# Latents loaded first, and the first three feature tiles multiplied in a written order

## The chip, the cores and the metric

The kernel runs on one core of a Trainium2 chip. Its engines have an instruction queue each: TensorE (PE, with a queue of its own for weight loads, PEld), VectorE (DVE), ScalarE (ACT), GpSimd (POOL) and SyncE (SP), which issues the loads. What is measured is the device time of one execution in microseconds (us).

## What is computed

Two layers of a backbone over 512 latent tokens and 256 context tokens, 1024 features wide, all in float32. Each layer begins with a normalisation that is modulated by a conditioning vector:

```python
shift, scale, gate = _adaln(c, ada_w[layer], ada_b[layer])
shift_c, scale_c, gate_c = _adaln(c_ctx, ada_w[layer], ada_b[layer])
h_l = _rmsnorm(x, norm_g[layer]) * (1.0 + scale[:, None]) + shift[:, None]
h_c = _rmsnorm(cx, norm_g[layer]) * (1.0 + scale_c) + shift_c
...
z = jnp.concatenate([h_c, h_l], axis=1) @ w_in
```

Layer 0 goes on with latent attention and a gated linear recurrence on z, layer 1 with neighbourhood attention. Only the start of layer 0 is touched here: the load of x and ctx, the two root-mean-squares, the modulation, and the first three 128-feature tiles of z.

## The kernel before

Features lie on the 128 partitions, tokens along the free axis: latents in columns 0 to 511 (`LAT`), context in 512 to 767 (`CTX`). The input is eight tiles `x_tiles[j]` of 128 x 768. Every matrix product is made of three float32r matmuls, high x high, high x low and low x high, so each operand is split in a high part (ACT copies) and a remainder (DVE subtracts); `split_raw` (L118 to L126) does that for weights.

The stage of the change goes in these steps.

`x_load` (L174) loads whole tiles; SP issues the loads in its queue's order. `norm0` (L356) squares each tile on ACT, adds the squares up in `acc0` on DVE, and at the last tile takes latents and context apart: `sq_sum` (L292) sums over the partitions on PE, `rs` (L311) makes the inverse root with one ACT root and five small DVE steps, `bc` (L318) broadcasts it by PE transposes, and ACT copies it to `rsb0`.

`ada_cols` (L242) makes modulation columns from weight chunks: `ada_mm` (L205) multiplies on PE (tile psada), ACT copies the rows, PE transposes them (psc), and DVE reduces and adds (`ashf`, `amul`). The first two input tiles have half chunks of their own (`ada_prep1`, `ada_go1`), the other six come in pairs from chunks 1 to 3 (`ada_prep`, `ada_go`), of which chunk ch needs the loads ch and ch + 4.

`hb(j, c)` (L403) makes the modulated input of tile j for latents (c = 0) or context (c = 1) by `h_block` (L335): DVE scales x by the column and the root, ACT adds the shift into `hh`, DVE takes the remainder `hl`.

`x_t(ft)` (L382) and `z_t` (L135) multiply: for each input tile k, three matmuls on the latents and three on the context, into one PSUM tile for each feature tile. psx0, psx1 and psg8 (weights w0t0, w0t1, w0t8) are the first three, psx2 (w0t2, started by the call behind this stage) is the fourth.

The order on each engine is made by a planner (`TC`, L20), which simulates the kernel and puts an instruction on its engine's queue when it is ready there, those written first going first. `behind(*engines)` (L198) pins what is written inside it behind the last instruction written so far on those engines. Buffers are tiles of pools: modulation weights have 8 (`t4a`), raw weights 3, their high parts and remainders 4 each.

Of the kernel before, what the change touches and what calls it, by code (L numbers as in the profile page):

```python
# [11 lines left out]
F32 = mybir.dt.float32  # L12
# [34 lines left out]
def build(nc, tc, A, out, dbg=None):  # L47
# [65 lines left out]
    def load_w(name, src, shape, new=None):  # L113
        raw = (new or t4)(name + "r", shape, F32, "r")
        SY.dma_start(raw, src)
        return raw
# [11 lines left out]
    def split_w(name, src, shape, new=None, eng=V, heng=S):  # L128
        return split_raw(name, load_w(name, src, shape, new), shape, new, eng, heng)

    def kfun(hl, n=None):
        h, l = hl
        return (lambda k: h[:, k], lambda k: l[:, k])
# [37 lines left out]
            for k in range(0, 8, step)  # L171
        ]

    def x_load(j):  # L174
        SY.dma_start(x_tiles[j], A["xin"][j])

    x_tiles = [px.tile([128, NT], F32, name=f"x{j}") for j in range(8)]
    ctt = cst.tile([128, 8, 2], F32, name="ctt")
# [19 lines left out]
    def behind(*engines):  # L198

        stack = ExitStack()  # L200
        for e in engines:
            stack.enter_context(tc.issue_after(next(i for i in reversed(nc.cur_bb.bb.instructions) if i.engine == e)))
        return stack
# [88 lines left out]
    def sq_sum(ps, sq, n, first, last):  # L292

        for i in range(0, n, 128):
            j = i // 64
            P.matmul(
                ps[:, j : j + 2], sq[:, i : i + 128], ones, start=(first and i == 0), stop=last,
                skip_group_check=True,
            )
# [26 lines left out]
    def rs_bc(name, ps, n, dst, pp, root=True):  # L326
        return bc(name, rs(name, ps, n, root), n, dst, pp)
# [21 lines left out]

    rsb0 = px.tile([128, NT], F32, name="rsb0")  # L350
    acc0 = px.tile([128, NT], F32, name="acc0")


    root = cst.tile([128, 1], F32, name="root")

    def norm0():  # L356
        sq = {}
        for j in range(8):
            sq[j] = th(f"sq{j}")
            S.activation(sq[j], x_tiles[j], AF.Square)  # L360
            if j == 4:
                S.activation(root, sq[0][:, 0:1], AF.Sqrt)
            for w in (LAT, CTX) if j == 7 else (slice(0, NT),):
                if j:
                    V.tensor_tensor(acc0[:, w], (acc0 if j > 1 else sq[0])[:, w], sq[j][:, w], ALU.add)
                if j == 7:
                    c = w is CTX
                    n, pp = (NL, NC)[c], (zz, zz3)[c]
                    ps = pp(f"pssum{c}")
                    sq_sum(ps, acc0[:, w], n, True, True)  # L370
                    if c == 0:
                        rs_bc("r00", ps, n, rsb0[:, w], pp)
                    else:
                        norm0c = lambda: rs_bc("r01", ps, n, rsb0[:, CTX], pp)
        return norm0c

    wt = {}

    def prep_t(ft):
        wt[ft] = kfun(split_w(f"w0t{ft}", A["w0t"][ft], (8, 128)))  # L380

    def x_t(ft):  # L382
        ps = zz(f"psx{ft}")
# [6 lines left out]
        ada_w[ch] = ada_load(0, ch, t4a)  # L390

    def ada_go(ch):
        for _ in ada_cols(0, 2 * ch, [ada_w.pop(ch), ada_w.pop(ch + 4)], paa):
            pass

    def ada_prep1(j):
        ada_w["half", j] = [[load_w(f"ada0{j}{m}", A["ada0"][j, m], (8, 128), t4a)] for m in range(2)]

    def ada_go1(j):
        for _ in ada_cols(0, j, ada_w.pop(("half", j)), paa, n=1):  # L400
            pass

    def hb(j, c):  # L403
        w = (LAT, CTX)[c]
        pc_ = [(lambda ap: ap, lambda ap: ap[:, w])]
        h_block(0, j, c, x_tiles[j][:, w], rsb0[:, w], hh[j], hl[j], pc_)
# [6 lines left out]
            going[key] = new  # L413
        next(going[key], None)

    psx = []
    for j in range(8):
        x_load(j)
    ada_prep1(0)
    norm0c = norm0()  # L420
    hh = [th(f"hh{j}", F32R) for j in range(8)]
    hl = [th(f"hl{j}", F32R) for j in range(8)]
    raw0 = load_w("w0t0", A["w0t"][0], (8, 128))
    ada_prep1(1)
    ada_go1(0)
    hb(0, 0)
    norm0c()
    with behind(PE, ACT):
        wt[0] = kfun(split_raw("w0t0", raw0, (8, 128)))
        hb(0, 1)  # L430
        ada_prep(1)
        ada_go1(1)
    hb(1, 0)
    hb(1, 1)
    ada_prep(5)
    ada_prep(2)
    ada_go(1)
    ada_prep(6)
    hb(2, 0)
    hb(2, 1)  # L440
    ada_prep(3)
    hb(3, 0)
    hb(3, 1)
    ada_prep(7)
    ada_go(2)
    hb(4, 0)
    hb(4, 1)
    ada_go(3)
    hb(5, 0)
    hb(5, 1)  # L450
    hb(6, 0)
    prep_t(1)
    hb(6, 1)
    hb(7, 0)
    hb(7, 1)
    prep_t(8)
    psx.append(x_t(0))
    psx.append(x_t(1))
    psg8 = zz3("psg8")
    z_t(both(psg8), wt.pop(8), hh, hl, 8)  # L460
    for j in range(8):
        dump(f"hh{j}", f(hh[j]))
        dump(f"hl{j}", f(hl[j]))
# [1375 lines left out]
```

## Time and profile before

| | us |
|---|---|
| median of 3 runs | 780.78 |
| lowest and highest run | 780.6, 781.55 |
| the profiled execution | 781.84 |
| its span, from first to last instruction | 780.0 |

One execution was recorded instruction by instruction. All times in rows are us from the start of the span, unless a row says ns. A line number is that of the program. A busy time says that an engine held an instruction, not that the instruction decided anything; what decides is read from the timelines, where "idle before" names what ended a wait.

### The profile page before, as it was taken

Reading aid. Unit: us, or ns where it says so; the run is one execution under the profiler, and the core shown is the slowest. Engines: PE = TensorE matmul, PEld = TensorE weight load, DVE = VectorE, ACT = ScalarE, POOL = GpSimd, SP = SyncE. Lnnn points to the kernel's source line nnn. Section 1 sums busy time; section 2 is a strip of 40 time slices with the busy share of each in tenths; the row PEclk is TensorE's granted clock in tenths of the full one; section 3 lists DMA queues with packets and bytes.
Section 4 is the critical chain, followed back from the end, with each engine's and each line's share of the span. In section 5 each row is a group of like instructions: output and inputs, shape, how many; then the busy total and the mean of one; then the engine's idle time right before and its main releaser. Section 6 shows DMA issues by size and latency. Waiting matters only on the chain.

```text
span 780.0 us, 13217 instructions
## 1 busy us (share of the span) xinstructions
PE 740.8 (95%) x4966; PEld 652.3 (84%) x4966; DVE 507.5 (65%) x1050; ACT 415.1 (53%) x810; POOL 164.8 (21%) x192
## 2 busy tenths in 40 slices
PE   2999999998999999999999999999999999999994
PEld 2678898887788877888998899889888799889994
DVE  5757599886478777653386467646653765568445
ACT  5434777954477777542344455445533644556533
POOL 0000002004154487404210023003200211022413
PEclk9999999999999999999999999999999999999998
DMA  8913413411455553256021541245125531436203
GB/s 322 408 58 109 134 50 100 165 39 38 118 155 158 166 160 119 89 196 236 28 82 59 149 145 29 82 125 173 59 78 162 166 105 55 111 100 169 82 1 108
DMA packets 33598, 95.29 MB, mean 122 GB/s; under 512 B 4608, under 2 KB 6784, under 8 KB 33536
## 3 DMA queue, kind: packets, MB, share of 16 engines
q1 hardware_dynamic: 32960, 93.93, 37.8%
q8 instruction: 39, 0.64, 0.3%
q10 hardware_dynamic: 576, 0.52, 0.2%
q14 instruction: 23, 0.19, 0.1%
HBM read 73.99 MB, written 4.19 MB: 100 GB/s over the span
## 4 chain that ended last, share of the span: by engine, by line
PE 75%; DVE 11%; ACT 5%; issue 3%; DMA 3%; SPq 1%; POOL 0%; DVEq 0%; ACTq 0%; POOLq 0%
PE psg L141 10%; PE psv L1270 8%; PE w0oy L1175 7%; PE psq L141 6%; PE w1oy L1175 6%; PE pskl L141 6%; PE psx L141 4%; PE pt L1387 3%; PE pskc L141 3%; PE s L808 3%; PE s L1346 2%; PE psada L215 2%; PE s L1347 2%; PE po L1370 2%; PE po L1371 2%
## 5 line engine op out<-in xcount | busy, mean ns | idle before, releaser
L764 POOL TENSOR_SCALAR p<-p,rc 128x512 f32<-128x512 f32 (+1 forms) x96 | 77.8, 813 | 323.7 <-DVE rc L763 309.7
L1354 ACT ACTIVATE p<-s,nm 128x512 f32<-128x512 f32 x64 | 43.8, 686 | 37.0 <-DVE nm L1352 20.9
L1390 DVE TENSOR_TENSOR ptl<-pt,pth 128x512 fp32r<-128x512 f32 x64 | 43.7, 688 | 26.7 <-ACT pth L1389 26.7
L1389 ACT ACTIVATE pth<-pt 128x512 fp32r<-128x512 f32 x64 | 37.3, 595 | 34.7 <-PE pt L1387 25.5
L1352 DVE CUSTOM_DVE_ANT_1 s<-s,bias 128x512 f32<-128x512 f32 x48 | 33.2, 696 | 16.5 <-PE s L1347 14.5
L1387 PE MATMUL pt<-ident,p 128*128 128x128 f32 x256 | 40.0, 272 | 0.0
L615 POOL TENSOR_TENSOR mix<-mix,la 128x256 f32<-128x256 f32 x4 | 3.6, 888 | 171.8 <-DVE la L609 123.6
L844 DVE TENSOR_TENSOR pt<-pt,pt 128x512 fp32r<-128x512 f32 x48 | 31.9, 681 | 11.5 <-ACT pt L843 11.3
L763 DVE RECIPROCAL rc<-rs 128x1 f32<-128x1 f32 x96 | 15.2, 158 | 32.7 <-ACT p L1354 23.6
L843 ACT ACTIVATE pt<-pt 128x512 fp32r<-128x512 f32 x48 | 27.4, 595 | 16.4 <-PE pt L881 16.2
L812 ACT ACTIVATE p<-s,nm 128x768 f32<-128x768 f32 x32 | 28.8, 901 | 11.7 <-DVE nm L810 11.5
L1346 PE MATMUL s<-k,q 128*128 128x256 f32 x128 | 34.3, 292 | 0.4 <-DMA q<-qx 0.2
L1387 PEld LDWEIGHTS pt<-ident,p 128*128 128x128 f32 x256 | 31.1, 140 | 4.0 <-issue 0.4
L810 DVE TENSOR_REDUCE nm<-s 128x1 f32<-128x768 f32 x32 | 30.4, 951 | 4.7 <-PE s L808 4.1
L1347 PE MATMUL s<-k,q 128*128 128x256 f32 x128 | 33.3, 284 | 0.0
L1370 PE MATMUL po<-pth,v 128*128 128x256 f32 (+1 forms) x96 | 31.7, 336 | 0.0
L1371 PE MATMUL po<-ptl,v 128*128 128x256 f32 (+1 forms) x96 | 29.6, 324 | 0.0
L881 PE MATMUL pt<-ident,p 128*128 128x128 f32 x192 | 28.7, 274 | 0.1
L862 PE MATMUL po<-pt,v 128*128 128x256 f32 x96 | 26.1, 296 | 1.9 <-DVE pt L844 1.8
L861 PE MATMUL po<-pt,v 128*128 128x256 f32 x96 | 26.6, 294 | 0.4 <-DVE rcc L763 0.4
L1346 PEld LDWEIGHTS s<-k,q 128*128 128x128 f32 x128 | 24.3, 190 | 3.1 <-issue 1.5
L1200 ACT ACTIVATE sq<-xr 128x512 f32<-128x512 f32 (+1 forms) x16 | 8.2, 522 | 33.1 <-DVE xr L1181 27.1
(966 smaller groups left out, 2635.3 us busy)
## 6 DMA issues: line engine op xcount, KB each, us to landing
ada_0r<-ada SPq DMA_DIRECT2D x22, 512.0 KB, 5.1
ada_4r<-ada SPq DMA_DIRECT2D x22, 512.0 KB, 5.4
q<-qx SPq DMA_DIRECT2D x32, 256.0 KB, 4.9
bias<-bias SPq DMA_DIRECT2D x16, 256.0 KB, 2.6
x<-xin SPq DMA_DIRECT2D x8, 384.0 KB, 6.4
xr<-xin SPq DMA_DIRECT2D x8, 384.0 KB, 7.0
x1d<-xr SPq DMA_DIRECT2D x8, 256.0 KB, 5.0
x<-x1d SPq DMA_DIRECT2D x8, 256.0 KB, 4.1
```

The source lines that it names most:

```text
L141: P.matmul(ps, a(k), b[k][:, c], start=(k == 0 and i == 0), stop=(k == nk - 1 and i == 2),)
L764: G.tensor_scalar(p, p, rc, 0.5, ALU.mult, ALU.mult)
L1175: P.matmul(ps, a, b[k][:, c], start=(n == m == 0 and ps is dst[0][0]), stop=(n == 7 and m == 2), skip_group_check=True,)
L1270: P.matmul(ps, tok(a[k], t), b[:, k % 4], start=(k == 0 and i == 0), stop=(k == 7 and i == 2))
L1346: P.matmul(s[:, :256], lhs, kap, start=(i == 0), stop=False, skip_group_check=True)
L1347: P.matmul(s[:, 256:], lhs, k2[:, CTX], start=False, stop=(i == 1), skip_group_check=True)
L1354: S.activation(p, s, AF.Exp, bias=nm, scale=-1.0, accum_out=rsum)
L1370: P.matmul(dst, vv, h, start=first, stop=False, skip_group_check=True)
L1371: P.matmul(dst, vv, l, start=False, stop=last, skip_group_check=True)
L1387: P.transpose(ps[:, 128 * j : 128 * j + 128], p1[hd, b][:, 128 * c : 128 * c + 128], ident)
L1389: S.activation(h, ps, AF.Copy)
L1390: V.tensor_tensor(l, ps, f(h), ALU.subtract)
```

## The change

Loads: the eight latent blocks (128 x 512) come first, then the weights of the first two modulation halves and of the first two feature tiles, and only then the eight context blocks (128 x 256), chunk 1 of the modulation, and the third feature tile's weights. Roots: `norm0` becomes two chains, one for the latents and one for the context, each with its own squares, adds, sums, root and broadcast; the context's squares get a tile of their own (`sqc`), and its sums lie in the PSUM slots of the modulation (`paa`). Matmuls: instead of `x_t` and `z_t`, which leave the order of the three feature tiles to the planner, `xk` multiplies one feature tile by named input tiles on latents or on context, and all of PE's work of this stage is pinned in the order in which it is written, the parts of the modulation in between (`go(key)` runs a modulation chunk to its next stop: first its matmuls, then its transposes).

```diff
+    def x_load(j, c):
+        w = (LAT, CTX)[c]
+        SY.dma_start(x_tiles[j][:, w], A["xin"][j][:, w])
...
+    def norm0(c):
+        n, w = (NL, NC)[c], (LAT, CTX)[c]
         for j in range(8):
-            sq[j] = th(f"sq{j}")
-            S.activation(sq[j], x_tiles[j], AF.Square)
...
+            sq = sqc[:, j] if c else th(f"sq{j}")[:, :NL]
+            S.activation(sq, x_tiles[j][:, w], AF.Square)
+            if j == 0:
+                prev = sq
+            else:
+                V.tensor_tensor(acc0[:, w], prev if j == 1 else acc0[:, w], sq, ALU.add)
+            if j == 0 and c == 0:
+                S.activation(root, sq[:, 0:1], AF.Sqrt)
+        ps = (zz, paa)[c](f"pssum{c}")
+        with behind(PE) if c else ExitStack():
+            sq_sum(ps, acc0[:, w], n, True, True)
+        r = rs(f"r0{c}", ps, n)
+        yield
+        with behind(PE):
+            bc(f"r0{c}", r, n, rsb0[:, w], (zz, paa)[c])
+        yield
...
+    def xk(ps, ft, c, js):
+        w, (wh, wl) = (LAT, CTX)[c], wt[ft]
+        with behind(PE):
+            for j in js:
+                for i, (a, b) in enumerate(((wh, hh), (wh, hl), (wl, hh))):
+                    P.matmul(
+                        ps[:, w], a(j), b[j][:, w], start=(j == 0 and i == 0), stop=(j == 7 and i == 2)
+                    )
...
     for j in range(8):
-        x_load(j)
+        x_load(j, 0)
     ada_prep1(0)
-    norm0c = norm0()
+    load0t(0)
+    ada_prep1(1)
+    load0t(1)
+    for j in range(8):
+        x_load(j, 1)
+    ada_prep(1)
+    ada_prep(5)
+    load0t(8)
+    n0, n1 = norm0(0), norm0(1)
+    next(n0)
+    go("h0", ada_go1(0))
+    go("h0")
+    next(n0)
...
+    with behind(DVE):
+        split0t(0)
     hb(0, 0)
...
+    go("h1", ada_go1(1))
+    go("h1")
     hb(1, 0)
...
+    split0t(1)
+    xk(psx[0], 0, 0, [0, 1])
+    xk(psx[1], 1, 0, [0, 1])
+    next(n1)
+    next(n1)
+    hb(0, 1)
     hb(1, 1)
-    ada_prep(5)
     ada_prep(2)
-    ada_go(1)
     ada_prep(6)
...
+    go("a1", ada_go(1))
+    with behind(DVE, ACT):
+        split0t(8)
+    xk(psx[0], 0, 1, [0, 1])
+    go("a1")
+    xk(psx[1], 1, 1, [0, 1])
...
+    for j in (2, 3):
+        for c in range(2):
+            hb(j, c)
+    for c in range(2):
+        xk(psg8, 8, c, [0, 1])
+    for i in (2, 3):
+        for c in range(2):
+            xk(psx[0], 0, c, [i])
+            xk(psx[1], 1, c, [i])
+        if i == 2:
+            go("a2", ada_go(2))
+    go("a2")
+    for c in range(2):
+        xk(psg8, 8, c, [2, 3])
+    for j in (4, 5):
+        for c in range(2):
+            hb(j, c)
+    go("a3", ada_go(3))
...
+    go("a3")
...
+    for i in range(2):
+        for c in range(2):
+            xk(psx[i], i, c, [6, 7])
+    for c in range(2):
+        xk(psg8, 8, c, [6, 7])
```

The lines left out multiply by input tiles 4 and 5 in the same manner, with chunk 3's transposes between the two.

## Rows read from the trace of the kernel before

**Rows 1.** The page: PE's busy us, share, instructions; its busy tenths by slice.
```profile
PE 740.8 (95%) x4966; PEld 652.3 (84%) x4966; DVE 507.5 (65%) x1050; ACT 415.1 (53%) x810; POOL 164.8 (21%) x192
...
PE   2999999998999999999999999999999999999994
```

**Rows 2.** Timeline of PE, 58 to 68: start, us, line, out<-in, count.
```profile
58.12 0.51 PE L141 MATMUL psg<-hh,w0t8l 128*128 128x512 f32 x2
58.75 0.58 PE L141 MATMUL psx<-hh,w0t2h 128*128 128x512 f32 x2
...
60.24 0.51 PE L141 MATMUL psx<-hh,w0t2h 128*128 128x512 f32 x2
...
67.66 0.35 PE L642 MATMUL psn<-w0n0h,hh 128*128 128x416 f32 x1
```

**Rows 3.** By stretch: length, busy (PE, PEld, DVE, ACT, POOL), PEclk, DMA share, GB/s.
```profile
23.30:28.80 5.50, 5.38 (x46) 3.06 (x47) 4.95 (x15) 2.86 (x7) 0.00 (x0) 1.00 1.03 401
28.80:35.00 6.20, 6.20 (x43) 4.15 (x43) 6.20 (x12) 3.10 (x5) 0.00 (x0) 1.00 1.03 411
35.00:43.00 8.00, 8.00 (x54) 5.94 (x53) 1.49 (x3) 1.28 (x2) 0.00 (x0) 1.00 0.86 344
```

**Rows 4.** Timeline of ACT and DVE, 9 to 21: squares, adds, root, its copy.
```profile
9.20 4.75 ACT L360 ACTIVATE sq<-x 128x768 f32<-128x768 f32 x5 [0.31 <-DMA x<-xin]
...
13.27 2.09 DVE L365 TENSOR_TENSOR acc<-acc,sq 128x768 f32<-128x768 f32 x3
...
17.49 0.27 ACT L304 ACTIVATE r00t<-pssumFalse,eps 128x4 f32<-128x4 f32 x1 [3.54 <-PE pssumFalse L296]
...
18.46 0.16 DVE L309 SCALAR_TENSOR_TENSOR r00r<-r00t,r00r 128x4 f32<-128x4 f32 x1
...
20.33 0.60 ACT L323 ACTIVATE rsb<-r00b 128x512 f32<-128x512 f32 x1 [0.74 <-PE r00b L322]
```

**Rows 5.** Timeline of DVE, 21 to 26: scaling, weight remainder, input remainder, columns.
```profile
21.72 1.15 DVE L338 SCALAR_TENSOR_TENSOR x<-x,am,rsb 128x512 f32<-128x512 f32 x2
...
22.79 1.22 DVE L125 TENSOR_TENSOR w0t0l<-w0t0r,w0t0h 128x1024 fp32r<-128x1024 f32 x1
...
23.92 1.14 DVE L341 SCALAR_TENSOR_TENSOR hl<-x,as,hh 128x512 fp32r<-128x512 f32 x2
...
24.98 0.17 DVE L234 TENSOR_REDUCE av<-psc 128x4 f32<-128x16 f32 x1
...
25.64 1.15 DVE L338 SCALAR_TENSOR_TENSOR x<-x,am,rsb 128x512 f32<-128x512 f32 x2
```

**Rows 6.** Timeline of PE: modulation halves, sums, broadcast, first feature matmul, chunk 1, transposes.
```profile
14.51 1.08 PE L215 MATMUL psada<-ada000r,c 128*32 128x128 f32 x16 [14.51 <-DMA ada000r<-ada]
...
15.52 1.87 PE L296 MATMUL pssumFalse<-ones,acc 128*128 128x2 f32 x8
...
19.18 1.12 PE L322 MATMUL r00b<-ident,r00r 128*128 128x128 f32 x4
...
21.60 0.61 PE L215 MATMUL psada<-ada011r,c 128*32 128x128 f32 x16
...
23.29 0.79 PE L141 MATMUL psx<-hh,w0t0h 128*128 128x512 f32 x2 [1.08 <-ACT hh L340]
...
24.11 0.64 PE L215 MATMUL psada<-ada_0r,c 128*32 128x256 f32 x8
...
24.57 0.61 PE L215 MATMUL psada<-ada_4r,c 128*32 128x256 f32 x8
...
46.61 0.38 PE L232 MATMUL psc<-ident,rows 128*128 128x128 f32 x2
```

**Rows 7.** DMA: packets from 7.5 to 12.5; one load (KB, us from issue to landing).
```profile
DMA packets 724, 2.03 MB, mean 406 GB/s; under 512 B 79, under 2 KB 79, under 8 KB 724
...
ada011r<-ada SPq DMA_DIRECT2D x1, 512.0 KB, 9.3
```

**Rows 8.** The scalings of x up to 60: ns least, median, most.
```profile
L338 DVE SCALAR_TENSOR_TENSOR x<-x,am,rsb x16: 476/612/752, 21.7 to 50.4; 128x512 f32<-128x512 f32 x8, 128x256 f32<-128x256 f32 x8
```

More of the change, by code (lines that the diff above doesn't have):

```diff
@@ L172, in ada_load @@
         ]
-    def x_load(j):
-        SY.dma_start(x_tiles[j], A["xin"][j])
+    def x_load(j, c):
+        w = (LAT, CTX)[c]
+        SY.dma_start(x_tiles[j][:, w], A["xin"][j][:, w])
     x_tiles = [px.tile([128, NT], F32, name=f"x{j}") for j in range(8)]
@@ L351, in build @@
     acc0 = px.tile([128, NT], F32, name="acc0")
+    sqc = px.tile([128, 8, NC], F32, name="sqc")
     root = cst.tile([128, 1], F32, name="root")
-    def norm0():
-        sq = {}
+    def norm0(c):
+        n, w = (NL, NC)[c], (LAT, CTX)[c]
         for j in range(8):
-            sq[j] = th(f"sq{j}")
-            S.activation(sq[j], x_tiles[j], AF.Square)
[L361 to L375, printed above, removed]
+            sq = sqc[:, j] if c else th(f"sq{j}")[:, :NL]
[14 more added lines that the diff above has]
+        yield
     wt = {}
@@ L392, in ada_go @@
     def ada_go(ch):
-        for _ in ada_cols(0, 2 * ch, [ada_w.pop(ch), ada_w.pop(ch + 4)], paa):
-            pass
+        return ada_cols(0, 2 * ch, [ada_w.pop(ch), ada_w.pop(ch + 4)], paa, True)
     def ada_prep1(j):
@@ L399, in ada_go1 @@
     def ada_go1(j):
-        for _ in ada_cols(0, j, ada_w.pop(("half", j)), paa, n=1):
-            pass
+        return ada_cols(0, j, ada_w.pop(("half", j)), paa, True, 1)
     def hb(j, c):
@@ L414, in go, with split0t, load0t @@
         next(going[key], None)
-    psx = []
+    def split0t(ft):
+        wt[ft] = kfun(split_raw(f"w0t{ft}", raw[ft], (8, 128)))
+    raw = {}
+    def load0t(ft):
+        raw[ft] = load_w(f"w0t{ft}", A["w0t"][ft], (8, 128))
     for j in range(8):
-        x_load(j)
+        x_load(j, 0)
     ada_prep1(0)
-    norm0c = norm0()
+    load0t(0)
[7 more added lines that the diff above has]
+    n0, n1 = norm0(0), norm0(1)
@@ L421, in build @@
+    next(n0)
+    go("h0", ada_go1(0))
+    go("h0")
+    next(n0)
     hh = [th(f"hh{j}", F32R) for j in range(8)]
     hl = [th(f"hl{j}", F32R) for j in range(8)]
-    raw0 = load_w("w0t0", A["w0t"][0], (8, 128))
-    ada_prep1(1)
-    ada_go1(0)
+    with behind(DVE):
+        split0t(0)
     hb(0, 0)
[L427 to L432, printed above, removed]
-    hb(1, 0)
+    go("h1", ada_go1(1))
@@ L434, in build @@
+    go("h1")
+    hb(1, 0)
+    psx = [zz("psx0"), zz("psx1")]
+    psg8 = zz3("psg8")
+    split0t(1)
[4 more added lines that the diff above has]
+    hb(0, 1)
     hb(1, 1)
-    ada_prep(5)
     ada_prep(2)
-    ada_go(1)
     ada_prep(6)
-    hb(2, 0)
-    hb(2, 1)
+    go("a1", ada_go(1))
[4 more added lines that the diff above has]
+    xk(psx[1], 1, 1, [0, 1])
     ada_prep(3)
-    hb(3, 0)
-    hb(3, 1)
@@ L444, in build @@
     ada_prep(7)
[L445 to L460, printed above, removed]
+    for j in (2, 3):
[9 more added lines that the diff above has]
+            go("a2", ada_go(2))
@@ new lines, in build @@
+    go("a2")
[6 more added lines that the diff above has]
+    for c in range(2):
+        xk(psx[0], 0, c, [4])
+        xk(psx[1], 1, c, [4])
+    go("a3")
+    for c in range(2):
+        xk(psx[0], 0, c, [5])
+        xk(psx[1], 1, c, [5])
+    for c in range(2):
+        xk(psg8, 8, c, [4, 5])
+    for j in (6, 7):
+        for c in range(2):
+            hb(j, c)
+    for i in range(2):
+        for c in range(2):
+            xk(psx[i], i, c, [6, 7])
@@ L461, in build @@
+    for c in range(2):
+        xk(psg8, 8, c, [6, 7])
+    wt.clear()
     for j in range(8):
```

## The prediction

> **What bounds the kernel now.** I began with the page's busy shares: TensorE (PE) is busy 95% of the span, and by the slices it is at 9 tenths everywhere but in the first [rows 1]. So an edit at the start is worth what it takes out of the first stage, if PE stays fed behind it. The stage ends, for my sum, where the fourth feature tile (psx2) does, since the first three and it are one unbroken run of PE work: at 67.66, with the first psn matmul [rows 2].
>
> The second view was busy time by stretch, around that start [rows 3]. From 23.3 PE is dense (5.38 of 5.5), and from 28.8 to 43 it has no idle time at all. In the same table VectorE (DVE) is the thing to watch: 4.95 of 5.5 from 23.3 and all of 6.2 from 28.8, and then 1.49 of 8 until 43. DVE is the second bound of this stage, hidden because PE always has something else queued.
>
> The timelines say what the start waits for. The squares on ScalarE (ACT) go at the pace of the input (five of 0.84 in 4.75), the adds on DVE end near 15.4 [rows 4], PE sums at 15.52, the inverse roots and their broadcast follow, the first modulation columns let DVE scale at 21.72, and the first feature matmul runs at 23.29 [rows 4 to 6]. Ahead of 14.51 PE does nothing.
>
> **The change, part by part.** *Loads.* 2.10 MB of latents replace 3.15 MB in front. The last whole tile landed by 13.1, where its square starts [rows 4]; the fourth had landed by 9.20, so 0.97 us a tile from there. By bytes, 2.10 MB is the end of the fourth tile and 1.3 more: 10.5. By number of rows moved (128 for each load, long or short) it would be up to 13.1. The queue moved 406 GB/s from 7.5 to 12.5, mostly with the same 3 KB rows [rows 7], and 401 to 411 later with 4 KB ones [rows 3], so bytes rule there: I take 11.0. Eight more issues of 0.33 to 0.5 us on SyncE (SP) are hidden: a load issued a little later landed 9.3 us after its issue [rows 7], the queue being full. If that cover went, 8 x 0.4 = 3 us would come back. [...]
>
> *Latent chain.* The 512-column add took 0.68 and the 256-column one 0.42 (2.09 for 768, 512 and 256 together, less 0.96) [rows 4]. Squares of 512 take some 0.6. Seven adds of 0.68 from 7.4 end at 12.2, against 14.9; PE can sum then (at 14.4 if the loads go by rows). In the written order PE then does sums (1.87), both halves of the first modulation columns (2 x 1.08 at this early pace, [rows 6]), the copy of the rows (0.3) and a transpose (0.42), and only then the broadcast (1.1). The columns are out on DVE by about 18.1, the broadcast copied by 19.1 (0.6, [rows 4]), against 21.7 and 20.9. A weight remainder, a scaling (below) and ACT's copy of 0.6 later the first feature matmul comes at 20.7, 2.6 earlier.
>
> *What DVE must do before chunk 1.* This is the step that decides. PE's order is now fixed: matmuls of input tiles 0 and 1 on latents for psx0 and psx1, then the sums of the context, its broadcast, and only then chunk 1's modulation matmuls, which before ran at 24.11 [rows 6]. The context sums therefore stand behind all of this on DVE, counted from 18.1 by start-to-start times [rows 5, 8]: two weight remainders of 1.13 (2.26); two scalings of 0.67 and two remainders of 0.67 (2.68; a latent and a context block together 1.07, split as their 0.75 and 0.48); the second columns (0.66); seven context adds of 0.42 (2.94). Sum 8.54. None can lie earlier: the first remainder is pinned behind the columns, the second weight lands past 18, and the context lands from about 18.7 to 21.3 (5.3 to 6.4 MB at 410 GB/s). So 26.6, with 0.3 of waits 26.9. The chain of the context then takes as long as it did: sums 1.0, root and five small steps 1.1, broadcast and its gap 0.8, 2.9 in all [rows 4 to 6]. Chunk 1 starts on PE at 29.8, although its data landed by 26. Moving its loads behind the context and the second weight therefore costs nothing; without that cover they would bind at 26.
>
> *PE from there.* One latent and one context matmul start 0.353 apart (21 such groups between 60.24 and 67.66) [rows 2]. Behind 29.8 lie 60 of those pairs (21.2), 12 context matmuls of 0.117 (1.4), three modulation chunks of 1.95 (four groups of eight, 0.46 apart) and three pairs of transposes of 0.35 (6.9) [rows 6]: 29.5. Holes: DVE starts chunk 1's columns behind two context blocks (0.2 at the context matmuls); the third weight's remainder (1.13) is pinned behind ACT's rows and comes out 0.7 after psg8 asks for it; input tile 2 needs its remainder, which the planner would again queue behind the scalings of two tiles (2 x 1.07), so 0.4 to 1.1 behind psg8's end. I take 1.3 for all. Before, PE filled such waits with any of the three tiles; the written order can't. For tiles 4 to 7 it leaves 4 us of other matmuls ahead, so no hole. The three tiles end at 60.6, against 58.45.
>
> *Given back.* psx0 ends 4.2 (12 pairs) before the stage does, and its weights' buffers go to the fourth tile, whose weights are then split in time. The 0.45 of gaps between its first matmuls (three groups took 1.49, [rows 2]) go: 24 pairs, 8.45. It ends at 69.05 against 67.66: **+1.4**. ACT gains 1.3 us of squares and DVE 0.9 of adds in all; ACT is idle half of that stretch (2.86 busy of 5.5, 3.10 of 6.2, [rows 3]). The root's table load stays behind the first square. The sums' new PSUM slots are shared with the columns, which are read by then. Nothing behind the fourth tile is edited, and PE's 95% [rows 1] lets the shift through.
>
> *The clock.* The 16 matmuls of half a load took 1.08 at 14.51 and 0.61 at 21.60 [rows 6], while the granted clock reads 1.00 in every stretch I read [rows 3]. Between 20.6 and 29.8 PE would now have about 5 us of work in 9. If it went back to the slow pace there, chunk 1 and what follows would take up to 1.7 longer. [...]
>
> **The rivals.** (1) *The early start carries through.* For: sums really come 3 us earlier, and if PE runs its columns at the later pace (0.95 less), DVE overlaps its list by 1 us, and the 1.3 of holes close, chunk 1 starts at 27.8 and 3.3 come back: 778.9. Against: the DVE list, which in the trace is as dense as can be [rows 3, 5]. It decides for a gain once chunk 1 starts before about 28.4. (2) *The latents land late, and slower for it.* Place: the first eight loads. If the queue goes by rows, they land at 13 instead of 11, and because every later step hangs on the first columns, all of the chain moves: +2.2 on the forecast, 784.4. It decides as soon as the last latent lands after 12, where DVE's adds no longer hide it. Against: the 406 GB/s with 3 KB rows. (3) *The clock falls* while PE waits for DVE: 783.9. (4) *The order changes nothing*, since the planner already mixes the three tiles [rows 2, 6] and PE was dense: then only the ends differ, 780.8.
>
> **How the numbers follow.** The profiled execution took 781.84, 1.84 more than its span of 780.0; the median of the runs shown is 780.78. Span 781.4, execution 783.2, and for the median 780.78 + 1.4 = 782.2. Own range: chunk 1 may start 1 earlier to 1.5 later, and holes 0.7 to 2, so 780.6 to 784. Chances: forecast 0.45, (1) 0.22, (2) 0.18, (3) 0.08, (4) 0.07. A measurement of this kernel tells about 0.2% (1.6 us) from no change: faster is below 779.2, slower above 782.3. The forecast lies almost on the second bound, so half of it counts as slower. Faster: most of (1), 0.20. Slower: 0.23 + 0.16 + 0.06 = 0.45. The rest, 0.35, is no change. The range takes in (1) and (2): 778.4 to 785.0.
>
> **What would show it.** In the changed profile: PE's first sums near 12 (loads by bytes) or 14 (by rows); first feature matmul near 20.7; DVE without a gap from 18 to 26.6; context sums on PE near 27 and chunk 1's modulation matmuls near 30; a hole of PE ahead of input tile 2's remainder; psx2's first matmul close on psg8's last, and its end near 69. I am wrong if chunk 1 runs before 28, which would mean that DVE's list was shorter or began earlier than counted, or if the shift at psx2's end isn't found at the end of the kernel.

## The result, and the profile after

The changed kernel took 791.56 us (median of four runs, 790.03 to 793.98) against 780.74 before: 1.0132 times as long, 95% interval 1.0113 to 1.0151. It is slower by 10.8 us, where 1.4 had been forecast. The four runs lie in two pairs, 790.0 twice and 793.08 and 793.98; the profiled execution is the last of these, with a span of 791.8 against 780.0.

Page of the changed kernel: busy us, share and instructions by engine; then PE's busy tenths and the granted clock in 40 slices. (PEld is TensorE too: the profile counts its weight loads in a row of their own.)

```profile
PE 746.8 (94%) x4966; PEld 658.9 (83%) x4966; DVE 508.1 (64%) x1056; ACT 416.3 (53%) x818; POOL 164.8 (21%) x192
...
PE   3799999899899998999999999999999999999994
...
PEclk9699999999999999999999999999999999999998
```

PE executes the same 4966 instructions as before and is busy 6.0 us longer [rows 1]; its low digits lie in the first two slices, up to 40 us, and so does the 6 of the clock. The PE timeline gives the chain of the start.

```profile
12.77 1.84 PE L297 MATMUL pssum<-ones,acc 128*128 128x2 f32 x8 [12.77 <-DVE sp L565]
...
21.57 0.33 PE L233 MATMUL psc<-ident,rows 128*128 128x128 f32 x1 [1.46 <-ACT rows L228]
21.66 0.48 PE L390 MATMUL psx<-hh,w0t0h 128*128 128x512 f32 x1
...
25.21 0.80 PE L390 MATMUL psx<-hh,w0t0h 128*128 128x512 f32 x1 [2.61 <-ACT hh L341]
...
29.16 0.63 PE L390 MATMUL psx<-hh,w0t1l 128*128 128x512 f32 x1
29.58 0.85 PE L297 MATMUL pssum<-ones,acc 128*128 128x2 f32 x4
31.73 0.66 PE L323 MATMUL r01b<-ident,r01r 128*128 128x128 f32 x2 [1.30 <-DVE r01r L310]
32.31 1.08 PE L216 MATMUL psada<-ada_0r,c 128*32 128x256 f32 x8
...
41.91 0.50 PE L390 MATMUL psx<-hh,w0t0h 128*128 128x512 f32 x1 [0.77 <-ACT hh L341]
43.27 0.50 PE L390 MATMUL psx<-hl,w0t0h 128*128 128x512 f32 x1 [0.86 <-DVE hl L342]
```

The sums come at 12.77 (15.52 before, [rows 6]) and the first feature matmul at 21.66 (23.29), so the early start is real. Then PE waits from 22.6 to 25.2 for the high part of input tile 1, works through nine latent matmuls (0.43 apart from the third on), and chunk 1's modulation begins at 32.31, 8.2 us later than before. The matmuls are long, 0.63 us and modulation groups of 1.08 where [rows 6] have 0.64: the stretches show why.

Stretches of the changed kernel; columns as in [rows 3], of which PE's busy time (first pair) and PEclk (third number from the end) matter.

```profile
19.50:22.20 2.70, 1.24 (x15) 0.76 (x8) 2.68 (x6) 2.70 (x9) 0.00 (x0) 1.00 1.02 338
22.20:25.20 3.00, 0.41 (x2) 0.00 (x0) 2.86 (x10) 1.57 (x4) 0.00 (x0) 0.77 1.00 367
25.20:29.20 4.00, 3.98 (x9) 2.81 (x10) 1.08 (x3) 0.00 (x0) 0.00 (x0) 0.50 1.01 373
29.20:32.30 3.10, 1.80 (x8) 1.33 (x6) 0.71 (x5) 0.26 (x1) 0.00 (x0) 0.50 1.03 403
32.30:37.50 5.20, 5.20 (x40) 3.00 (x40) 1.76 (x4) 2.71 (x6) 0.00 (x0) 0.50 0.99 375
37.50:43.00 5.50, 3.90 (x22) 2.75 (x20) 5.13 (x11) 2.57 (x5) 0.00 (x0) 1.00 0.96 336
43.00:50.00 7.00, 6.73 (x48) 4.55 (x49) 1.67 (x4) 0.70 (x2) 0.00 (x0) 0.76 0.23 91
```

PE is busy 0.41 of 3 us from 22.2, and in that stretch the granted clock falls from 1.00 to 0.50. It stays there until about 37.5, and falls again (0.76 from 43 to 50) behind the next holes (3.90 busy of 5.50), those ahead of input tile 2. Every stretch of [rows 3] read 1.00. In that first stretch the mean of 0.77 puts the fall near 23.8, 1.2 us into the wait.

The first psn matmul (psn is the product that follows psx2) stands at 76.6 instead of 67.66 [rows 2]: 8.9 us of the 11.8 by which the spans differ. The rest arises far behind, at 145 us. PE's waits there for lgl, the remainder of a gate's weights in the recurrence, between 136 and 152, first of the kernel before, then of the changed one (us in total, times, longest):

```profile
PE pg L141 <- DVE lgl L565: 0.8, 1, 0.8
```

```profile
PE pg L141 <- DVE lgl L617: 3.2, 1, 3.2
```

No line of that part was edited. VectorE has its work in another order there: the planner had another start to go by.

### The profile page after: what moved, and what is told of

It is laid out like the page before. It is cut to its first block, busy times and chain, and to the rows that moved or that the text cites. A ratio compares the mean times of both kernels' runs of the same rounds, so it can differ in the third digit from the quotient of the medians.

```text
span 791.8 us, 13243 instructions
## 1 busy us (share of the span) xinstructions
PE 746.8 (94%) x4966; PEld 658.9 (83%) x4966; DVE 508.1 (64%) x1056; ACT 416.3 (53%) x818; POOL 164.8 (21%) x192
## 4 chain that ended last, share of the span: by engine, by line
PE 77%; DVE 12%; ACT 5%; issue 3%; DMA 2%; POOL 0%; SPq 0%; DVEq 0%; ACTq 0%; POOLq 0%
PE psg L141 9%; PE psv L1322 8%; PE w0oy L1227 7%; PE psq L141 6%; PE w1oy L1227 6%; PE pskl L141 6%; PE pt L1439 3%; PE psada L216 3%; PE pskc L141 3%; PE s L860 3%; PE psx L390 3%; PE psx L141 2%; PE s L1398 2%; PE s L1399 2%; PE po L1422 2%
## 5 line engine op out<-in xcount | busy, mean ns | idle before, releaser
L1406 ACT ACTIVATE p<-s,nm 128x512 f32<-128x512 f32 x64 | 43.8, 686 | 37.4 <-DVE nm L1404 20.7
L1442 DVE TENSOR_TENSOR ptl<-pt,pth 128x512 fp32r<-128x512 f32 x64 | 43.6, 687 | 26.4 <-ACT pth L1441 26.3
L1404 DVE CUSTOM_DVE_ANT_1 s<-s,bias 128x512 f32<-128x512 f32 x48 | 33.3, 696 | 16.6 <-PE s L1399 14.5
L815 DVE RECIPROCAL rc<-rs 128x1 f32<-128x1 f32 x96 | 15.2, 158 | 31.8 <-ACT p L1406 21.6
L864 ACT ACTIVATE p<-s,nm 128x768 f32<-128x768 f32 x32 | 28.9, 902 | 11.3 <-DVE nm L862 11.1
L1423 PE MATMUL po<-ptl,v 128*128 128x256 f32 (+1 forms) x96 | 29.6, 324 | 0.0
L1398 PEld LDWEIGHTS s<-k,q 128*128 128x128 f32 x128 | 24.3, 190 | 3.2 <-issue 1.7
```

Source lines behind the costliest of these rows:

```text
L1398: P.matmul(s[:, :256], lhs, kap, start=(i == 0), stop=False, skip_group_check=True)
L1404: V.tensor_tensor_reduce(sv, sv, bb, -1.0, 3e38, ALU.add, ALU.min, nm)
L1406: S.activation(p, s, AF.Exp, bias=nm, scale=-1.0, accum_out=rsum)
L1442: V.tensor_tensor(l, ps, f(h), ALU.subtract)
```

## The experiments

Twelve further runs were made; e5_again is the change once more, unaltered. All are read by the same marks of their profiled execution: the start of chunk 1's modulation, the first psn matmul, the stretch from the last psn matmul to the first of pskr (transposes of psn's result; the stretch holds the wait for lgl), and the mean granted clock from 20 to 50. The column "before" is the median of the kernel before in the same series of runs.

| run | us | before | ratio, 95% | chunk 1 | psn | psn to pskr | clock 20 to 50 |
|---|---|---|---|---|---|---|---|
| kernel before | 780.78 | | | 24.1 | 67.7 | 64.3 | 1.00 |
| the change | 791.56 | 780.74 | 1.0113–1.0151 | 32.3 | 76.6 | 68.0 | 0.72 |
| e2_chains | 786.59 | 781.44 | 1.0049–1.0082 | 29.3 | 73.6 | 64.4 | 0.83 |
| e3_order | 787.98 | 781.44 | 1.0066–1.0096 | 31.4 | 72.4 | 67.9 | 0.89 |
| e4_chunk1 | 792.11 | 781.44 | 1.0119–1.0150 | 30.2 | 74.8 | 67.7 | 0.83 |
| e1_filled | 788.74 | 781.44 | 1.0078–1.0108 | 31.0 | 71.5 | 67.0 | 0.94 |
| e7_warm | 788.69 | 781.94 | 1.0061–1.0120 | 31.7 | 72.3 | 68.0 | 1.00 |
| e5_again | 789.64 | 781.71 | 1.0069–1.0113 | 32.5 | 76.9 | 66.5 | 0.72 |
| e8_lgl | 786.18 | 781.94 | 1.0038–1.0071 | 32.2 | 72.8 | 64.4 | 0.89 |
| e11_before_lgl | 781.66 | 781.71 | 0.9988–1.0007 | 24.0 | 67.5 | 62.8 | 1.00 |
| e6_adds | 788.59 | 781.94 | 1.0068–1.0114 | 31.3 | 71.9 | 66.6 | 0.89 |
| e10_pesum | 787.28 | 781.71 | 1.0057–1.0117 | 30.7 | 72.8 | 64.3 | 0.83 |
| e9_all | 786.95 | 781.94 | 1.0042–1.0075 | 31.3 | 71.9 | 64.1 | 1.00 |
| e12_best | 789.42 | 781.47 | 1.0093–1.0129 | 29.9 | 70.4 | 65.2 | 0.94 |

### Which part of the change costs: e2, e3, e4

**e2_chains** keeps the new loads and the two root chains, and leaves the order of all matmuls to the planner.

```diff
-    xk(psx[0], 0, 0, [0, 1])
-    xk(psx[1], 1, 0, [0, 1])
...
+    for ps, ft in ((psx[0], 0), (psx[1], 1), (psg8, 8)):
+        z_t(both(ps), wt[ft], hh, hl, 8)
```

> The first half of the change alone: latents loaded first and the two root chains, but the three feature tiles, the modulation and the roots in the order that the planner finds, nothing pinned. Clock theory and order theory: PE always finds some feature matmul, no wait over 2 us, psx2 ends at 66 to 69, time 779 to 782. Load theory (the split loads and the late context are what costs): psx2 ends at 73 or later, time 787 to 791.

Measured: 1.0065 times the kernel before. The planner's order leaves the same hole. PE timeline:

```profile
23.27 0.50 PE L141 MATMUL psx<-hh,w0t0h 128*128 128x512 f32 x1 [3.06 <-ACT hh L341]
23.61 0.40 PE L141 MATMUL psx<-hh,w0t1h 128*128 128x512 f32 x1
26.36 1.02 PE L297 MATMUL pssum<-ones,acc 128*128 128x2 f32 x4 [2.36 <-DVE acc L367]
```

PE waits 3.06 for ACT and 2.36 for the context's adds, and the granted clock reads 0.50 from 24 to 34. Split loads and a split norm lose time without the written order: 5.9 us at psn's start.

**e3_order** keeps the loads and the one norm of the kernel before, and has the written order alone.

```diff
     for j in range(8):
-        x_load(j, 0)
+        x_load(j)
     ada_prep1(0)
+    norm0c = norm0()
...
-    next(n0)
+    hb(0, 0)
+    norm0c()
```

> The second half alone: whole tiles loaded first and one chain of squares as in the kernel before, but the first three feature tiles and chunks 1 to 3 in the written order. Clock theory: both blocks of input tiles 0 and 1 are there by 28 and chunk 1's data by 24, so PE waits under 2 us at a time, the clock stays up, psx2 ends at 68 to 70, time 781 to 784. Order theory: as the changed kernel, psx2 at 74 or later, time 787 to 791.

Measured: 1.0081. Here the context's root is in time, but the written order waits too (26.74, 1.75 us for input tile 1, where the planner of the kernel before had run chunk 1), the clock is at 0.50 from 26 to near 33, and the stretch from psn to pskr is the long one. So neither part is harmless, and both have a wait of PE ahead of chunk 1.

```profile
26.74 0.79 PE L388 MATMUL psx<-hh,w0t0h 128*128 128x512 f32 x1 [1.75 <-ACT hh L340]
```

**e4_chunk1** is the change with chunk 1's modulation matmuls ahead of the context's sums.

```diff
     xk(psx[1], 1, 0, [0, 1])
+    go("a1", ada_go(1))
     next(n1)
     next(n1)
...
-    go("a1", ada_go(1))
```

> The changed kernel with chunk 1's modulation matmuls put ahead of the context's sums on PE. Clock theory: the wait at 22.2 stays as it is, the clock falls at 25 all the same, chunk 1 runs at the slow pace but 3 us earlier; psx2 ends at 73 to 76, time 787 to 791. Order theory (chunk 1 behind the context's chain is what costs): psx2 ends at 70 to 72, time 784 to 786.

Measured: 792.11 (790.68 to 792.69), no gain and above both ranges. In the profiled run, the fastest, chunk 1 starts 2.1 us earlier, and psn 1.8 earlier than in the profiled change, which by what e5_again shows below says little. Behind it the context's sums come at 32.13 instead of 29.58, and PE then waits 1.30 for the root and 1.53 for the first context block. The wait is moved, not removed: what is late is the context's chain, whichever of the two goes first.

### The clock: e1, e7, e5

**e1_filled** adds 25 unused matmuls where PE waits.

```diff
+    def warm(ps, n):
+        with behind(PE):
+            for _ in range(n):
+                P.matmul(ps, wt[0][0](0), hh[0][:, LAT], start=True, stop=True, skip_group_check=True)
...
-    xk(psx[0], 0, 0, [0, 1])
+    xk(psx[0], 0, 0, [0])
+    warm(psg8[:, LAT], 11)
+    xk(psx[0], 0, 0, [1])
```

> The changed kernel with 25 matmuls added that nothing uses, put into three places where PE only waits: 11 between input tiles 0 and 1 of psx0, 7 between the context's sums and its broadcast, 7 ahead of input tile 2. They keep PE at work and move nothing else. Clock theory (PE waits 3.0 us for DVE at 22.2, its clock falls to the lower level, and all its work runs at half pace from 25 to 37): granted clock 1.00 up to 40, psx2's last matmul ends at 69 to 71 instead of 76.6, time 783 to 787. Order theory (the written order itself leaves PE without work, the clock is a side show): psx2 ends at 75 or later, time 789 or more.

Measured: 1.0093 (788.74), psn at 71.5, both between the two theories. The clock fell all the same:

```profile
19.50:22.00 2.50, 0.67 (x11) 0.46 (x4) 2.50 (x5) 2.50 (x8) 0.00 (x0) 1.00 0.89 263
22.00:26.00 4.00, 4.00 (x12) 3.19 (x11) 3.84 (x13) 1.75 (x5) 0.00 (x0) 0.57 1.00 376
26.00:30.00 4.00, 4.00 (x21) 3.31 (x20) 0.79 (x5) 0.26 (x1) 0.00 (x0) 1.00 1.00 362
```

PE held matmuls without a gap from 21.6, and the clock was low from about 22.6 to 26; the wait that went ahead of it was that for the second columns (busy 0.67 of 2.50). I took the first wait to count as well as the one that I had filled.

**e7_warm** fills that one too, with matmuls that need only the first weights (29 unused ones in all).

```diff
+    warm(psg8[:, LAT], 6)
     go("h1")
```

> The changed kernel with 29 unused matmuls of 128 x 512 added on TensorE where it waits: 6 behind the second modulation half, 11 ahead of input tile 1, 5 between the context's sums and their broadcast, 7 ahead of input tile 2; they read only the first weights, so they can run from 19.9 on. Clock theory: the granted clock stays at 1.00 from 20 to 50; chunk 1's modulation starts near 30.5 and takes 1.9 instead of 3.6; psn's first matmul near 70 (76.6 without the fillers, 71.5 with the earlier fillers that still let the clock fall at 22.8), the later stall of the fourth gate remainder stays (about 3 us of wait instead of 0.8), in all 785 to 787 us. Rival (the written order and the late chain cost by themselves, whatever the clock): psn at 73 or later, 789 us or more.

Measured: the granted clock is 1.00 from 20 to 140, and yet psn starts at 72.3 and the kernel takes 1.009 times the time before. Part of the expectation held (chunk 1's modulation takes 1.9 instead of 3.6 us) and its size did not: with the clock kept up, psn is still 4.6 us later than in the kernel before, of 8.9. The fillers themselves are the measure of the holes (PE timeline):

```profile
22.60 0.27 PE L233 MATMUL psc<-ident,rows 128*128 128x128 f32 x1
...
23.41 2.69 PE L437 MATMUL psg<-w0t0h 128*128 128x512 f32 x11
26.81 0.50 PE L390 MATMUL psx<-hh,w0t0h 128*128 128x512 f32 x1 [0.72 <-ACT hh L341]
...
29.55 0.50 PE L297 MATMUL pssum<-ones,acc 128*128 128x2 f32 x4
29.91 1.40 PE L437 MATMUL psg<-w0t0h 128*128 128x512 f32 x5
31.35 0.41 PE L323 MATMUL r01b<-ident,r01r 128*128 128x128 f32 x2
31.69 0.64 PE L216 MATMUL psada<-ada_0r,c 128*32 128x256 f32 x8
```

Chunk 1 starts at 31.69 although every matmul from 20 on runs at a granted clock of 1.00: PE waits for VectorE and ScalarE, and here the faster PE only waited longer. The holes are 3.4 us ahead of input tile 1 (2.6 in the profiled change), 1.4 ahead of the broadcast (1.3) and 1.9 ahead of input tile 2's remainder (1.6).

The 4.6 are not all the kernel's own. The latents' sums began at 13.34 here (and in e8), 0.6 later than in the profiled change. And the fillers delay what they measure: the transpose of the second columns waits behind six of them until 22.60, though ACT had copied its rows by 22.1, VectorE then reduces these columns behind two adds, and input tile 1's scaling comes at 25.26 instead of 23.66, 1.0 later than the late begin explains. With both set off, I estimate that some 3 us of the 8.9 would remain at a clock that never falls. (In e1, whose sums began at 12.74 and whose clock was low for 3.4 us, 3.8 remain.)

**e5_again** is the change unaltered.

> The changed kernel unaltered, once more. Its four runs lay in two pairs, 790.0 and 793 to 794 us, and the profiled one was of the upper pair; the mend behind the fourth tile (which alters nothing ahead of 120 us) showed a granted clock that rose again at 30 us instead of 37.5, and psn's first matmul at 72.8 instead of 76.6. Theory (the same program falls into two courses of the clock in this stage, some 3.5 us apart): a profile of the lower course would show psn at 72.5 to 73, one of the upper at 76 to 77, and the runs lie near 790 and near 793.5 again. Rival (the two pairs are noise of another place): psn at 76.6 whatever the run takes.

Measured: 793.11 in the profiled run, 788.23 to 789.89 in four others. The profile is again of the upper pair's kind (psn at 76.9, mean clock 0.72 from 20 to 50). Of the nine runs of the change three took 793 to 794 us, with a mean granted clock of 0.981 or 0.982 over the whole span, and six took 788.2 to 790.0, with 0.987 to 0.989. So the two groups are two courses of the clock, upper and lower. No profile of the change itself fell in the lower one; but e8_lgl, which has the same instructions ahead of 120 us, ran through a lower course:

```profile
22.80:25.80 3.00, 0.38 (x3) 0.01 (x1) 2.86 (x10) 1.55 (x4) 0.00 (x0) 0.55 0.98 354
25.80:30.00 4.20, 4.20 (x9) 3.03 (x10) 1.06 (x3) 0.00 (x0) 0.00 (x0) 0.51 1.02 369
30.00:34.00 4.00, 2.71 (x39) 1.55 (x38) 1.83 (x8) 1.43 (x4) 0.00 (x0) 1.00 1.03 408
34.00:43.00 9.00, 7.07 (x42) 5.47 (x38) 7.49 (x16) 4.42 (x8) 0.00 (x0) 1.00 1.02 406
43.00:50.00 7.00, 7.00 (x71) 5.24 (x74) 2.38 (x8) 1.39 (x3) 0.00 (x0) 1.00 0.16 61
```

The clock falls sooner here, near 23.1 by the mean of 0.55, just as the wait begins (23.8 in the profile of the change), and it is up again at 30 instead of 37.5 and doesn't fall a second time. That is 3.8 us at psn's start (72.8 against 76.6), and the groups of the change's runs are 3 to 6 us apart. The sizes agree in the clock too: 0.72 against 0.89 over 30 us is 5.1 us of full clock, which over 790 us makes 0.0065, about what lies between 0.981 and 0.988. That the change's faster runs went through just this course of e8 is likely from these sizes, and not shown.

The price of the low clock is read against e7, where it read 1.00 from 20 to 140. As the rows stand, it is 0.5 us in the lower course (psn at 72.8 against 72.3), since PE would have waited for VectorE anyhow, and 4.3 in the upper. With e7's own delays set off (1.0, and for the upper course the late begin of 0.6 too) I estimate 1.5 and 5.9. The clock came up again at 30 in e8, where PE had been busy 4.20 of 4.20 us from 25.8, and at 37.5 in the change, busy 5.20 of 5.20 from 32.3. What decides between the two courses is not shown.

### Behind the fourth tile: e8, e11

**e8_lgl** pins one later step behind lgl; nothing ahead of 120 us is altered.

```diff
+        last_lgl[:] = [i for i in nc.cur_bb.bb.instructions if i.engine == DVE][-1:]
...
-    nat_norm(0)
+    with tc.issue_after(last_lgl[0]):
+        nat_norm(0)
```

> The changed kernel with the third normalisation of the token-wise part (nat_norm(0)) pinned on its engines behind the remainder lgl of the fourth gate, so that lgl leaves VectorE about 2 us earlier; nothing ahead of 120 us is touched. Theory (a part of the loss arises behind the fourth tile, from another planned order): the wait of TensorE for lgl falls from 3.2 to about 1.2 us and the dip of the clock behind it goes; pskr comes 2 to 3 us earlier than the 191.2 of the changed kernel, in all 788.5 to 789.5 us. Rival (the stall only moves, because VectorE or ScalarE is late there anyway): 791 to 792 us.

Measured: 786.18, better than expected; its four runs lie close together (785.87 to 787.35), where those of the change lie in pairs. PE's wait:

```profile
PE pg L141 <- DVE lgl L619: 1.4, 1, 1.4
```

The stretch from psn to pskr is 64.4, as in the kernel before (64.3). The table gives the price better than one run does: the kernels with a wait of 3.1 or 3.2 for lgl (the change, e1, e3 to e7) have 66.5 to 68.0 there, those with 0.8 to 1.4 (before, e2, e8, e9, e10, e12) 64.1 to 65.2. Every kernel with the written order and without the pin has it, e2 with the planner's order hasn't.

**e11_before_lgl** is the kernel before with the same pin.

> The kernel before with nat_norm(0) pinned behind lgl, alone: what that pin is worth where TensorE waits only 0.8 us for lgl. Theory (the stall of 3.2 us belongs to the changed kernel, the pin gains only what it removes there): within 0.2% of the kernel before, 780 to 782 us. Rival (the pin is a gain of its own, which would make it no measure of the loss): 778.5 us or less.

Measured: 0.9998 (0.9988 to 1.0007). The stretch to pskr shrinks to 62.8 here, but w0oy's first matmul then starts at 320.1 instead of 318.8: the gain is given back. So the pin is worth nothing to the kernel before, and the 2 to 4 us that it gives the changed one are most simply read as a loss that the change had made. (What the pin alters behind pskr, 2.9 us here, is not explained.)

### VectorE's list: e6, e10

**e6_adds** puts the context's seven adds behind input tile 1's remainder.

```diff
+    split0t(1)
     hb(1, 0)
...
-    split0t(1)
...
-    next(n1)
+    with behind(DVE):
+        next(n1)
     next(n1)
```

> The changed kernel with the context's seven adds written behind the remainder of input tile 1 on VectorE, so that nothing stands between the second modulation columns and the scaling of that tile. Both theories: the high part of input tile 1 comes about 1.1 us earlier (24.1 instead of 25.2), and TensorE's wait ahead of it shrinks from 3.0 to about 1.8 us; the context's sums come at 28 instead of 29.2. Theory A (what costs is that the clock falls, and a wait this short no longer lets it fall): granted clock 1.00 from 20 to 40, psn's first matmul near 70 instead of 76.6, about 785 us. Theory B (any wait near 1.8 us lets it fall as the 3.0 did, as in the run of the written order alone): granted clock 0.50 again from about 24 on, psn near 75, 789 to 790 us. Rival (the clock is not the cause, the lateness of the chain is): only the 1.1 comes off, 790.4 us.

Measured: input tile 1 at 24.52 (25.21), the wait ahead of it 1.87 instead of 2.61, and the clock low none the less. The stretch from 22 to 24 holds the fall:

```profile
22.00:24.00 2.00, 0.65 (x3) 0.21 (x2) 1.30 (x5) 1.35 (x5) 0.00 (x0) 0.68 1.01 377
```

A mean of 0.68 over 2 us puts the fall near 22.7. The shortened wait had only begun then (PE's matmuls of tile 0 end at 22.65), so this run doesn't decide between theories A and B: as in e1 and e8, the wait that lies ahead of the fall is that for the second columns (1.81 here). The clock is back by 29.6. The median (788.59) is near B's; psn starts at 71.9, between the two. Chunk 1 comes 1.0 earlier than in the profiled change, the context's sums at 28.88.

**e10_pesum** (with the pin of e8) takes the adds off VectorE; PE sums the squares of all eight tiles.

```diff
+            S.activation(sqc[:, j], x_tiles[j][:, CTX], AF.Square)
+            with behind(PE):
+                sq_sum(ps, sqc[:, j], NC, j == 0, j == 7)
```

> The changed kernel with the pin on nat_norm(0), and the context's squares summed over the eight tiles by TensorE itself (16 small matmuls, those of the first two tiles ahead of the second columns' transpose, the others between input tiles 0 and 1 on psx0), so that VectorE's seven context adds (2.94 us) are gone. Theory (VectorE's list decides when the context's root, and so chunk 1, can come): the high part of input tile 1 at 24.1 instead of 25.2, the context's sums done at 26 instead of 29.6, chunk 1's modulation starts at 28 to 29 instead of 32; psn's first matmul at 69 to 70 (72.8 with the pin alone), in all 782 to 783.5 us against 786.2. Rival (the small matmuls take TensorE as long as the adds took VectorE, or the clock's fall decides by itself): psn at 72 or later, 785.5 us or more.

Measured: 787.28 (785.45 to 792.52; the profiled run is the fastest), no gain over e8. PE timeline:

```profile
22.39 4.37 PE L297 MATMUL pssum<-ones,sqc 128*128 128x2 f32 x24
26.62 0.77 PE L403 MATMUL psx<-hh,w0t0h 128*128 128x512 f32 x1
...
30.34 0.38 PE L323 MATMUL r01b<-ident,r01r 128*128 128x128 f32 x2
30.66 0.64 PE L216 MATMUL psada<-ada_0r,c 128*32 128x256 f32 x8
```

The 24 small matmuls between input tiles 0 and 1 took 4.37 us, more than the adds they replace (2.94), under a clock that fell to 0.50 near 23.2 (mean 0.80 from 22 to 24, 0.50 from 24 to 30) although PE held instructions all the time from 21.5. The rival holds for the time. Of the theory one part is left: chunk 1 starts 1.5 earlier than in e8 (0.9 if e8's later begin is set off), close behind the nine latent matmuls.

### All at once: e9, e12

**e9_all** joins e6, e7 and e8, with 25 fillers: 6, 7, 5 and 7. Of the two groups of 5 that the expectation names, only the one behind the context's sums is in the kernel.

> The changed kernel with the three mends together: fillers (6, 7 ahead of input tile 1, 5 ahead of and 5 behind the context's sums, 7 ahead of input tile 2), the context's adds behind input tile 1's remainder, and nat_norm(0) behind lgl. If the three causes are all: granted clock 1.00 from 20 to 50, psn's first matmul near 69.5 (67.7 before the change), wait for lgl near 1.2 us, 781.5 to 784 us. If the order itself gains once the clock holds: below 780. If something else is lost that I haven't named: 786 or more.

Measured: 786.95, clock 1.00, wait for lgl 1.2, and psn at 71.9, not 69.5. The third case: something else is lost. The PE timeline shows a part of it:

```profile
27.64 0.39 PE L390 MATMUL psx<-hh,w0t1l 128*128 128x512 f32 x1
29.11 0.58 PE L297 MATMUL pssum<-ones,acc 128*128 128x2 f32 x4 [1.07 <-DVE acc L367]
```

With the adds behind input tile 1, PE is done with the latents at 28 and waits for the adds; with the adds ahead of it (the change), the adds are done at 26.3 and PE waits for input tile 1. The sums come at 29.1 here, and at 29.6 in e7, where the clock is up as well: whichever goes first on VectorE, the other is late. With the clock up, that list and the matmuls between it and the sums are what chunk 1 waits for.

**e12_best** shortens that list by e10's sums (half of them behind input tile 1), has 8 fillers to hold the clock and the pin of e8, and pins input tile 3's scalings behind input tile 2's remainders.

```diff
-    for j in (2, 3):
+    for c in range(2):
+        hb(2, c)
+    with behind(DVE):
         for c in range(2):
-            hb(j, c)
+            hb(3, c)
```

> The run with the context's sums on TensorE, with the three remaining losses of this stage taken away too: 8 unused matmuls of 128 x 512 (3 behind the second modulation half, 2 between the context's sums, 3 ahead of input tile 2) so that the clock holds, half of the sums moved behind input tile 1 on psx0, and the scalings of input tile 3 pinned behind the remainders of input tile 2 on VectorE. Theory (late chain, clock, planned order behind the fourth tile: with all three mended the early start is worth what my first rival said): granted clock 1.00 from 20 to 60, chunk 1's modulation at 27.5 to 28.5, wait ahead of input tile 2's remainder below 0.3 instead of 0.87 us, psn's first matmul at 68 to 68.5 (67.7 in the kernel before), 781 to 782.5 us. Rival 1 (the clock falls all the same, since the small sums don't hold it): granted clock 0.50 between 23 and 30, psn at 71 or later, 785 us. Rival 2 (the early start carries through): psn ahead of 67, below 780 us.

Measured: 789.42 (786.98 to 791.32), above every range that was expected; the profiled run is the fastest. In it chunk 1 starts at 29.87, input tile 2's remainder is 0.29 late instead of 0.86, and psn starts at 70.4, the earliest with the change in it and still 2.7 behind the kernel before. The clock fell late, behind the sums (0.76 from 26 to 30), as in rival 1. And the gain did not arrive at the end: w0oy's first matmul stands at 323.6 in e12 and in e8, though psn lies 2.4 apart. Between pskr and w0oy the variants take 138.2 to 142.0 us (139.1 before) without an edit there; what lies there takes back as much as the mends give, and its cause was not sought. No variant beats the kernel before.

## Why the prediction was wrong

**Held.** The latents came by bytes: the eight latent squares follow each other to 11.1, so the last block had landed by 10.5 (11.0 taken, up to 13.1 by rows). These 256 KB blocks did not cost the 2.2 us of rival 2. The 128 KB context blocks did move more slowly: 341 GB/s from 18.4 to 20.3, where 640 of 657 packets are under 2 KB, and 338 from 19.5 to 22.2, where the last of the blocks land, with the DMA engines fully busy (1.02), against 401 to 411 in [rows 3]. PE's sums came at 12.77 (12.2), the columns at 18.07 (18.1), the broadcast was copied at 18.9 (19.1), and the last context add ended at 26.3 (26.6). Rival 2 fell with the loads, rival 4 with e3, which has the written order and is slower.

**First step that failed: where the list stands.** The sum of 8.54 us on VectorE was right (8.2 from 18.07 to 26.28); what was wrong is that the context's sums were put directly behind it. PE's own queue has nine latent matmuls ahead of the sums, and they begin only with input tile 1. The planner put the adds between the steps that lead to that tile. VectorE's timeline in the changed kernel:

```profile
21.67 0.42 DVE L367 TENSOR_TENSOR acc<-sqc 128x256 f32<-128x256 f32 x1
22.00 0.17 DVE L235 TENSOR_REDUCE av<-psc 128x4 f32<-128x16 f32 x1
22.19 0.42 DVE L367 TENSOR_TENSOR acc<-acc,sqc 128x256 f32<-128x256 f32 x1
...
23.32 0.42 DVE L367 TENSOR_TENSOR acc<-acc,sqc 128x256 f32<-128x256 f32 x1
23.66 0.75 DVE L339 SCALAR_TENSOR_TENSOR x<-x,am,rsb 128x512 f32<-128x512 f32 x1
...
25.20 0.75 DVE L342 SCALAR_TENSOR_TENSOR hl<-x,as,hh 128x512 fp32r<-128x512 f32 x1
25.86 0.42 DVE L367 TENSOR_TENSOR acc<-acc,sqc 128x256 f32<-128x256 f32 x1
```

The columns of tile 1 are reduced at 22.00 and used at 23.66; four adds lie around the small steps between. With the adds last instead (e9) the list has waits in it, and runs to 29. So the sums come at 29.6, not 26.9, and chunk 1 at 32.3, not 29.8. The order alone makes the smaller part of that: from input tile 1 (25.2) to the sums it took 4.4 us at the low clock, and 2.7 in e7 with the clock up, and from the sums to chunk 1 2.7 and 2.1 (2.9 in the forecast). By these rows the sums would have come near 27.9 and chunk 1 near 30.1 with the clock up, an estimate; 1.1 of the first miss is the order's and 1.6 the clock's. A smaller miss of the same kind: the first feature matmul, at 21.66 instead of 20.7, stands on PE behind the transpose of the second columns, whose rows ACT copied only after two squares of the context.

**Second, and the larger in the profiled run: the clock.** The sum has it at nothing. Rival 3 named the place and the fall of the clock, and was given 0.08 and 1.7 us. Its price at psn was 0.5 to 4.3 as the rows stand, and about 1.5 (lower course) to 5.9 (upper) by the estimate with e7's own delays set off, because the 0.50 outlasted the wait: in the upper course nine latent matmuls, the whole of chunk 1 (3.6 instead of 1.9) and part of the next stretch ran at it. No row read from the trace of before shows a clock below 1.00; that was a reason for a wide bound, not for a small chance, once the forecast itself contained 4 us of idle PE. (The two paces that the prediction took its 1.7 us from, 1.08 and 0.61, both lie where the recorded clock reads 1.00, at 14.5 as at 21.6, so the record didn't show them as two clocks.)

**Third: "nothing behind the fourth tile is edited".** True of the text, not of the order. The planner works on the whole kernel, PE's wait for lgl grew from 0.8 to 3.2, and the stretch from psn to pskr took 3.7 us more in the profiled change.

**The terms.** Holes ahead of psg8's and input tile 2's matmuls were put at 1.3; they are 0.24 + 0.77 + 0.86 = 1.9. In e7, where the clock plays no part, chunk 1 starts 1.9 later than forecast; 0.6 of that are the run's later begin and about 1.0 its fillers' delay, so 0.3 are left. From there to psn it takes 40.6 against the forecast's 39.25 (69.05 less 29.8), 1.4 more, 0.6 of it the holes. With the 1.4 of the forecast itself that makes about 3 us at psn's start, and with the clock (1.5 or 5.9) 4.5 in the lower course, its late begin set off, and 8.9 in the upper. Up to psn's end 1.1 comes back (0.7 of it a wait that PE has in the kernel before alone). The lgl wait and its wake add 2 to 4. These shares are estimates, since no run has the change's own begin, no filler and a clock that holds. They account for the size of the loss, not for each tenth of it: the differences of 1 to 3 us between pskr and w0oy remain without a cause of their own.

**The rival that gained** (1) had the right condition, chunk 1 ahead of 28.4. No variant met it; the earliest with split loads was 29.3 (e2). What the early start would be worth if it were met stays untried.

## What to carry to other kernels

Where an engine's order is written out by hand, draw the chain through all queues to the next instruction that it can't pass, not only down the busiest engine: here a list of VectorE was counted, and the nine matmuls that stood between it and its user were not. Behind waits of 1.8 to 3.1 us in the dense PE stretch here, ahead of chunk 1, the granted clock read 0.50 for 3.4 us (e1) to 13.7 us (the change), so price such a wait by its own length and by rows at both clocks, and give that case a real chance. And where a planner orders the rest of the kernel, an edit at the start has an error of some us at the end, in both directions, that no row of the edited stretch shows.

## What the runs showed of the hardware beyond that

The same instructions ran through this stage in two ways 3.8 us apart: granted clock 0.50 from 23.1 to 30 (e8), or from 23.8 to 37.5 and once more from 44 to 48 (the change). PE did the same work up to the fall in both, 0.6 us apart, and yet the fall came as the second wait began in one and 1.2 us into it in the other. In e1 the clock fell while PE had no gap, behind an earlier wait (0.57 from 22 to 26, PE busy 4.00 of 4.00, behind a wait of 1.8), and in e10 without such a wait (PE busy 1.56 of 2.00 from 20 to 22, 2.00 of 2.00 from 22 to 24, with a mean clock of 0.80), while PE held nothing but sums of 128 x 2 for 4.4 us. The early pace remains unexplained: the 16 modulation matmuls at 14.5 took 1.08 before and after the change while the granted clock read 1.00. A group of chunk 1 with as many columns took 1.08 at 0.50 in the change and 0.61 to 0.64 at 1.00 in e7; what made the early groups as slow as those at 0.50 is not shown. This early pace also ended sooner where the clock fell sooner: the last group of the second modulation half (start 19.0 to 19.6) still took 1.08 in the two profiles of the change, with the fall at 23.8 and 24.3, and 0.65 to 0.72 in e1, e6 and e8, with the fall at 22.6 to 23.1, though e1 and e6 began their sums within 0.1 of the change. The first fillers of e7 ran 0.33 apart from 20.6, against 0.23 from 23.4 on.
